# GpSimd's sums and differences of two SBUF operands moved to VectorE and ScalarE, three waits reordered

## The chip, the cores and the metric
The kernel runs on one core of a Trainium2 chip. The metric is the device time of one execution in microseconds; the time before is the median of three runs. PE (TensorE) multiplies matrices, VectorE (DVE in the rows) and GpSimd (POOL) and ScalarE (ACT) work element by element, and SyncE (SP) issues most transfers. PE's clock has two levels, 1.2 and 2.4 GHz; the profile gives the granted clock as a share of the higher one.

## The reference, cut to what matters
One inference step of a two-layer hybrid backbone for 640 tokens (512 latent ones and 128 of context) at width 1024, all in fp32:
```python
def modulate(x, g, shift, scale):
    return rmsnorm(x, g) * (1 + scale) + shift

def mixer_front(h, p):
    z = h @ p['w_in']
    a_b, a_c, a_x, sgu_uv, cq, ckv, k_pe, sq, sk, sv = split_in_proj(z)
    y_conv = a_b * dwconv_centred(a_c * a_x, p['conv_w'])
    y_sgu = chunk_sgu(sgu_uv, p['sgu_norm'], p['sgu_w'], p['sgu_b'])
    ...

def mix_latent(h, p, ckv_ctx, kpe_ctx, k_ctx, v_ctx):
    ...
    return jnp.concatenate([y_conv, y_sgu, y_mla, y_swa], axis=-1) @ p['w_out']

def squared_relu_mlp(h, w1, w2):
    return jnp.square(jax.nn.relu(h @ w1)) @ w2

def trunk_layer(x, mod, p, mix_fn):
    shift1, scale1, gate1, shift2, scale2, gate2 = jnp.split(mod, N_MOD, axis=-1)
    y, ctx_state = mix_fn(modulate(x, p['norm1'], shift1, scale1))
    x = x + gate1 * y
    x = x + gate2 * squared_relu_mlp(modulate(x, p['norm2'], shift2, scale2), p['w1'], p['w2'])
    return x, ctx_state
```
`mod` is silu(c) @ w_ada + b_ada, one vector of six parts for the latent tokens and one for the context. The MLP is 4096 wide. In sgu the second half of gelu(z) is normalised and mixed over chunks of 128 tokens by four matrices, and multiplies the first half. MLA and the windowed attention rotate parts of their queries and keys by position.

## The kernel before
**Precision.** Every fp32 operand of a product is kept as a high part, rounded to a shorter format, and a low part, the difference. `mm3` then makes three matrix products: high x high (L248), high x low (L249), low x high (L250). A weight unit is loaded by `load_unit`: a transfer into one of three raw buffers, the high part on ScalarE (L239), the low part (L240) on VectorE, or on GpSimd where `pool` is set, into one of four `hl` buffers. `split` (L253, L254) does the same for values made in the kernel.

**Layout.** Activations stand with features on the partitions, x as 128 x 8 x 640, and are worked through in two halves of 384 and 256 tokens. The result of a product stands in PSUM; banks come from three pools of two, `bank` takes the first two pools in turn and `bank2` the third.

**Order.** A scheduler puts each engine's instructions in one order when the program is built; an engine then works through its own list, and waits where an operand or a buffer isn't free yet. What stands ahead of an instruction on its engine is thus set beforehand.

**Start.** The sums of squares of x are made, then the normalised x (`xr`, L319, eight products of two SBUF operands on VectorE). The modulation vectors come from two sources: ada tiles, a 128x1024 weight block which two reductions on VectorE (L174) multiply with the two conditioning vectors and sum; and `AdaRows`, products on PE (`adar`, L198) of weights (`adan`, transfers L311 and L327) that are transposed back (`adat`, L210). Gains (L184), scaling on ScalarE and the low part of h (L337) follow. Then the first products of the input projection start.

**Attention half.** Three `tm_block` calls make token-major projections (`tm`), each with four weight units; in layer 0 their low parts are made on GpSimd. `tm_rstd` (L480, L482) makes the power -1/2 of the row norms on GpSimd. After that come sgu (four products, each evacuated by L582 on VectorE), the feature-major projection tiles (`fm`), rotation of queries and keys (L636 to L639), the windowed attention (the scaling by 1/sum is L731 on GpSimd), MLA (L942 subtractions, scaling L968), and the output projection `out`. Each of its tiles is added to x with a gate by `gate_add` (L428), which then adds the tile's squares to the norm's sum (L269 square on ScalarE, L270 sum).

**Second norm and MLP.** `Modulate.step` makes h per feature block and half: L358 scales x (VectorE), L365 makes the high part (ScalarE), L369 the low part (VectorE). The MLP begins with four W1 units loaded ahead (`head`, low parts on GpSimd) and two `Pair`s of hidden tiles: relu (L1140) and its square rounded (L1141) on ScalarE, the square in fp32 (L1145), and the low part (L1146). In layer 0 the remaining hidden tiles follow in `two_plain`, and the second product in `mlp2`; between them stand ada tiles for later use. Layer 1 makes part of its products by a block scheme with fewer products (`mod.sums` makes the sums of blocks that it needs).

## Time and profile before

| what | value |
|---|---|
| median of 3 runs | 1538.87 us (1536.42 to 1539.4) |
| the profiled execution, its own time | 1542.1 us |
| its span, first to last instruction | 1540.2 us |
| mean granted PE clock | 0.978 |

The rows further down come from the profiled execution, and its own time is what they add up to; it is 3.2 us above the median. In a row of grouped instructions the line is the kernel's line, "out<-in" names the tiles, x the number of instructions, and the first numbers after the bar are the busy time in us and the mean of one in ns. In a timeline the first column is the time since the start of the span and the second the duration; "[7.92 <-DMA ...]" is the idle time ahead of the instruction and what ended it.

### The profile page before, as it was taken

How to read it: one execution, taken by the hardware profiler on the slowest of the kernel's cores; microseconds unless marked ns; L12 is line 12 of the kernel's file. 1: busy time of each engine (PE TensorE's matmuls, PEld its weight loads, DVE VectorE, ACT ScalarE, POOL GpSimd, SP SyncE). 2: the span in 40 equal slices, each digit the busy share in tenths (PEclk: the TensorE clock that was granted, in tenths of full speed). 3: DMA queues.
4: the chain of work that ended last, by engine and by line, in shares of the span. 5: the costliest groups of instructions: out<-in, count | busy, mean ns of one | idle time of the engine just before them, and what ended most of it. 6: DMA issues, size and time to landing. Idle time of an engine off the chain costs nothing.

```text
span 1540.2 us, 25201 instructions
## 1 busy us (share of the span) xinstructions
PE 1477.7 (96%) x9716; PEld 1418.2 (92%) x9716; DVE 1129.9 (73%) x2210; ACT 668.4 (43%) x1400; POOL 242.9 (16%) x245
## 2 busy tenths in 40 slices
PE   6899999989999999999999999999999999999997
PEld 3798988889999999999999989898999999999996
DVE  5988877869978778776457666687886676566655
ACT  3544556744322322322236545675745244334422
POOL 2132103243210110110120120132300000000002
PEclk9899999999999999999999999999999999999999
DMA  8544321333654445444211411111223223222211
GB/s 312 202 134 139 99 67 35 102 101 100 204 161 155 151 139 163 151 150 138 80 49 57 128 43 35 36 49 45 83 69 96 69 83 96 62 76 96 84 55 69
DMA packets 50103, 160.22 MB, mean 104 GB/s; under 512 B 6208, under 2 KB 10304, under 8 KB 49984
## 3 DMA queue, kind: packets, MB, share of 16 engines
q1 hardware_dynamic: 48320, 154.68, 31.3%
q10 hardware_dynamic: 1664, 3.93, 0.7%
q8 instruction: 77, 1.26, 0.3%
q14 instruction: 42, 0.34, 0.1%
HBM read 155.55 MB, written 3.05 MB: 103 GB/s over the span
## 4 chain that ended last, share of the span: by engine, by line
PE 77%; DVE 10%; ACT 5%; issue 3%; POOL 1%; DMA 1%; POOLq 0%; DVEq 0%; ACTq 0%
PE w L250 13%; PE w L249 13%; PE w L248 13%; PE qcd L248 2%; PE fm L248 2%; PE qcd L250 2%; PE qcd L249 2%; PE fm L250 2%; PE fm L249 2%; PE out L248 2%; PE tm L249 2%; PE tm L248 2%; PE tm L250 2%; PE out L250 2%; PE out L249 2%
## 5 line engine op out<-in xcount | busy, mean ns | idle before, releaser
L248 PE MATMUL w<-u,hl 128*128 128x384 f32 (+1 forms) x1024 | 317.4, 310 | 5.7 <-DVE x L428 3.4
L249 PE MATMUL w<-u,hl 128*128 128x384 f32 (+1 forms) x1024 | 317.3, 310 | 0.7 <-DVE u L1198 0.7
L250 PE MATMUL w<-u,hl 128*128 128x384 f32 (+1 forms) x1024 | 317.1, 310 | 0.4 <-DVE hl L240 0.4
L239 ACT CAST hl<-raw 128x1024 fp32r<-128x1024 f32 (+3 forms) x176 | 170.6, 972 | 261.7 <-PE w L250 156.2
L240 DVE TENSOR_TENSOR hl<-raw,hl 128x1024 fp32r<-128x1024 f32 (+3 forms) x156 | 183.2, 1177 | 53.0 <-ACT hl L239 52.4
L428 DVE SCALAR_TENSOR_TENSOR x<-w,mod,x 128x128 f32<-128x128 f32 (+1 forms) x384 | 155.0, 434 | 73.1 <-PE w L250 71.8
L248 PEld LDWEIGHTS w<-u,hl 128*128 128x128 f32 x1024 | 194.6, 190 | 6.5 <-DVE x L428 3.6
L249 PEld LDWEIGHTS w<-u,hl 128*128 128x128 f32 x1024 | 194.8, 190 | 1.0 <-DVE u L1198 1.0
L250 PEld LDWEIGHTS w<-u,hl 128*128 128x128 f32 x1024 | 194.6, 190 | 0.6 <-DVE hl L240 0.6
L249 PE MATMUL w<-h,hl 128*128 128x384 f32 (+1 forms) x576 | 179.2, 313 | 3.6 <-DVE h L369 3.6
L250 PE MATMUL w<-h,hl 128*128 128x384 f32 (+1 forms) x576 | 179.4, 312 | 0.0
L248 PE MATMUL w<-h,hl 128*128 128x384 f32 (+1 forms) x576 | 179.0, 312 | 0.0
L174 DVE CUSTOM_DVE_ANT_0 junk<-adaw,cb,vec 128x1024 f32<-128x1024 f32 x84 | 110.5, 1317 | 28.2 <-DMA adaw<-in_wada 28.0
L270 POOL TENSOR_TENSOR ss<-ss,sq 128x384 f32<-128x384 f32 (+1 forms) x40 | 37.3, 932 | 504.7 <-ACT sq L269 503.9
L174 DVE CUSTOM_DVE_ANT_0 adaw<-adaw,cb,vec 128x1024 f32<-128x1024 f32 x84 | 114.2, 1359 | 1.1
L249 PEld LDWEIGHTS w<-h,hl 128*128 128x128 f32 x576 | 110.3, 192 | 4.8 <-DVE h L369 4.8
L1145 POOL TENSOR_TENSOR rq<-rr 128x384 f32<-128x384 f32 (+1 forms) x64 | 61.9, 969 | 334.2 <-ACT rr L1140 310.3
L248 PEld LDWEIGHTS w<-h,hl 128*128 128x128 f32 x576 | 110.5, 192 | 0.0
L250 PEld LDWEIGHTS w<-h,hl 128*128 128x128 f32 x576 | 110.3, 192 | 0.0
L248 PE MATMUL fm<-h,hl 128*128 128x256 f32 (+1 forms) x288 | 93.4, 324 | 2.1 <-DVE u L582 2.1
L249 PE MATMUL fm<-h,hl 128*128 128x256 f32 (+1 forms) x288 | 90.7, 315 | 0.0
L250 PE MATMUL fm<-h,hl 128*128 128x256 f32 (+1 forms) x288 | 90.6, 315 | 0.0
(329 smaller groups left out, 3404.6 us busy)
## 6 DMA issues: line engine op xcount, KB each, us to landing
raw<-in_wf SPq DMA_DIRECT2D x146, 512.0 KB, 3.5
adaw<-in_wada SPq DMA_DIRECT2D x84, 512.0 KB, 3.6
raw<-in_wo SPq DMA_DIRECT2D x24, 384.0 KB, 3.0
adan<-in_wnat SPq DMA_DIRECT2D x12, 512.0 KB, 8.3
raw<-in_wt SPq DMA_DIRECT2D x16, 384.0 KB, 3.3
x<-in_xT ACTq DMA_DIRECT2D x4, 640.0 KB, 7.2
raw<-in_wt SPq DMA_DIRECT2D x8, 288.0 KB, 3.0
raw<-in_wo SPq DMA_DIRECT2D x4, 512.0 KB, 3.6
```

The lines of the kernel that those rows point to most:

```text
L174: nc.vector.tensor_tensor_reduce(out=raw if g else junk, in0=raw, in1=cb[:, g, :], op0=ALU.mult, op1=ALU.add, scale=1.0, scalar=vecs[l][:, ...
L239: nc.scalar.copy(hl[:, 0, :n], raw[:, :n])
L240: (nc.gpsimd if pool else nc.vector).tensor_sub(hl[:, 1, :n], raw[:, :n], f(hl[:, 0, :n]))
L248: nc.tensor.matmul(out, lhsT=lhs[0], rhs=rhs[0], start=start, stop=False, skip_group_check=more)
L249: nc.tensor.matmul(out, lhsT=lhs[0], rhs=rhs[1], start=False, stop=False, skip_group_check=more)
L250: nc.tensor.matmul(out, lhsT=lhs[1], rhs=rhs[0], start=False, stop=stop, skip_group_check=more)
L270: (nc.gpsimd if pool else nc.vector).tensor_add(self.s[:, t0:t0 + n], self.s[:, t0:t0 + n], sq[:, :n])
L428: nc.vector.scalar_tensor_tensor(out=x[:, m, t0:t0 + n], in0=ps[:, t0 - b0:t0 - b0 + n], scalar=mods[l][g][:, gate + m:gate + m + 1], in1= ...
L1145: nc.gpsimd.tensor_mul(q, r, r)
```

## The change
All operations on GpSimd that take two SBUF tensors of some width are moved: the low parts of `load_unit` (20 on GpSimd before: eight of 768 columns and four of 576 in layer 0's `tm_block`, eight of 1024 in the `head` of both layers), the sums of the norm (20 of 384 columns and 20 of 256), the first product of the rotation (six), and the subtractions in MLA's queries (sixteen) go to VectorE. The 64 squares of layer 0's MLP go to ScalarE. The powers (L295, L482), four copies and the scalings by 1/sum (L731, L968) stay on GpSimd. Three orders change too: sgu puts two heads into one tile of the third PSUM pool; in `two_plain` of j = 1, seven ada tiles in place of eight are spread as (2, 2, 2, 1), and the last one comes later; in layer 1 the first W2 unit is loaded ahead of the block sums and handed to `mlp2`.

```diff
--- before.py
+++ after.py
@@ -232,12 +232,12 @@
                 ada_tile(*t, pool)
 
 
-    def load_unit(src, n=1024, pool=False):
+    def load_unit(src, n=1024):
         raw = rawp.tile([128, 1024], F32, tag="raw", name=nm("raw"))
         nc.sync.dma_start(out=raw[:, :n], in_=src)
         hl = hlp.tile([128, 2, 1024], F32R, tag="hl", name=nm("hl"))
         nc.scalar.copy(hl[:, 0, :n], raw[:, :n])
-        (nc.gpsimd if pool else nc.vector).tensor_sub(hl[:, 1, :n], raw[:, :n], f(hl[:, 0, :n]))
+        nc.vector.tensor_sub(hl[:, 1, :n], raw[:, :n], f(hl[:, 0, :n]))
         return hl
 
     def transpose(out, src):
@@ -261,13 +261,13 @@
             self.rb = None
             self.s = tp([128, TOK], "ss")
 
-        def add(self, k, t0, n, pool=False):
+        def add(self, k, t0, n):
             if k == 0:
                 nc.scalar.activation(self.s[:, t0:t0 + n], x[:, k, t0:t0 + n], AF.Square)
                 return
             sq = tmp2([128, 384], "sq")
             nc.scalar.activation(sq[:, :n], x[:, k, t0:t0 + n], AF.Square)
-            (nc.gpsimd if pool else nc.vector).tensor_add(self.s[:, t0:t0 + n], self.s[:, t0:t0 + n], sq[:, :n])
+            nc.vector.tensor_add(self.s[:, t0:t0 + n], self.s[:, t0:t0 + n], sq[:, :n])
 
         def start(self):
 
@@ -430,7 +430,7 @@
                 scalar=mods[l][g][:, gate + m:gate + m + 1], in1=x[:, m, t0:t0 + n],
                 op0=ALU.mult, op1=ALU.add)
         if norm is not None:
-            norm.add(m, *HALVES[half], m < 6)
+            norm.add(m, *HALVES[half])
 
 
     def layer(l, h, next_norm, nxt):
@@ -451,7 +451,7 @@
 
         def tm_block(srcs, kn, cols, evac):
             seq = (0, 1, 3, 2) if l == 0 else (0, 1, 2, 3)
-            us = {i: load_unit(srcs[i], kn * cols, l == 0) for i in seq}
+            us = {i: load_unit(srcs[i], kn * cols) for i in seq}
             ks = [i * kn + k for i in seq for k in range(kn)]
             if l == 0:
                 ada_steps(4, tt)
@@ -575,7 +575,9 @@
         ws = load_unit(wkvs[l, :, 512:1024], 512)
         wsH, wsL = (ws[:, s, 0:512].rearrange("p (h q) -> p h q", h=4) for s in range(2))
         for hd in range(4):
-            ps = bank("sgu")
+            if hd % 2 == 0:
+                two = bank2("sgu")
+            ps = two[:, hd % 2, :]
             d0 = 64 * hd
             mm3(ps[:, :320], (wsH[:, hd, :], wsL[:, hd, :]),
                 (vhl[0][:, :, d0:d0 + 64], vhl[1][:, :, d0:d0 + 64]), True, True)
@@ -634,7 +636,7 @@
             if i == 2:
                 nc.sync.dma_start(out=o_k[l], in_=xc[:, 2, :])
             nc.vector.stream_shuffle(out=tmp, in_=raw, mask=[z ^ 16 for z in range(32)])
-            nc.gpsimd.tensor_mul(raw, raw, rs[:, 0, :])
+            nc.vector.tensor_mul(raw, raw, rs[:, 0, :])
             nc.vector.tensor_mul(tmp, tmp, rs[:, 1, :])
             nc.vector.tensor_add(raw, raw, tmp)
             if i < 2:
@@ -939,7 +941,7 @@
                 for i in range(2):
                     r = ROPE[i]
                     nc.scalar.copy(qq[i][r, 0, t0:t0 + e], rot[r, :e])
-                    nc.gpsimd.tensor_sub(qq[i][r, 1, t0:t0 + e], rot[r, :e], f(qq[i][r, 0, t0:t0 + e]))
+                    nc.vector.tensor_sub(qq[i][r, 1, t0:t0 + e], rot[r, :e], f(qq[i][r, 0, t0:t0 + e]))
                     r = NOPE[i]
                     nc.scalar.activation(qq[i][r, 0, t0:t0 + e], pq[0][r, :e], AF.Copy, scale=MLA_SCALE)
                     nc.vector.scalar_tensor_tensor(
@@ -1139,10 +1141,7 @@
                 hh = ui[:, 0, t0:t0 + n]
                 nc.scalar.activation(r, ps[:, :n], AF.Relu)
                 nc.scalar.activation(hh, r, AF.Square)
-                if blocks:
-                    nc.scalar.activation(q, r, AF.Square)
-                else:
-                    nc.gpsimd.tensor_mul(q, r, r)
+                nc.scalar.activation(q, r, AF.Square)
                 nc.vector.tensor_sub(ui[:, 1, t0:t0 + n], q, f(hh))
 
             def load(self):
@@ -1237,7 +1236,7 @@
                 for half in range(2):
                     two[i // 2].plain([w, w], i % 2, half)
                 if l == 0:
-                    ada_steps((3, 3, 2, 0)[i] if j == 1 else 1)
+                    ada_steps((2, 2, 2, 1)[i] if j == 1 else 1)
             return two[0].u + two[1].u
 
         def mlp2_tile(ut, u, m, half, nrm):
@@ -1248,10 +1247,10 @@
                 mm3(ps[:, :n], (u[:, 0, c0:c0 + 128], u[:, 1, c0:c0 + 128]), act(ut, k, t0, n), k == 0, k == 3)
             gate_add(ps, m, half, l, 40, nrm)
 
-        def mlp2(j, ut):
+        def mlp2(j, ut, first=None):
             if j < 7:
                 for i in range(4):
-                    u = load_unit(wf[l, U_W2 + 4 * j + i])
+                    u = first if i == 0 and first else load_unit(wf[l, U_W2 + 4 * j + i])
                     for m in (2 * i, 2 * i + 1):
                         for half in range(2):
                             mlp2_tile(ut, u, m, half, None)
@@ -1269,7 +1268,7 @@
                     nxt.step(half, k)
 
         head = [Pair(p, None if blocks else [ta([128, 2, TOK], "u") for _ in range(2)]) for p in range(2)]
-        ws = [load_unit(wf[l, U_W1 + i], pool=True) for i in range(4)]
+        ws = [load_unit(wf[l, U_W1 + i]) for i in range(4)]
         for half in range(2):
             for i in range(4):
                 head[i // 2].plain(ws[2 * (i // 2):2 * (i // 2) + 2], i % 2, half)
@@ -1278,9 +1277,10 @@
                         mod.step(1, k)
         us = head[0].u + head[1].u
         if blocks:
+            first = load_unit(wf[l, U_W2])
             for s in range(4):
                 mod.sums(s)
-            mlp2(0, us)
+            mlp2(0, us, first)
             us = full(2) + full(3)
             for j in range(1, 8):
                 if j < 7:
```

The line numbers after the change are two higher from sgu on, and one lower than before behind the squares of the MLP.

The first place is VectorE's list at the start, right behind the eight L319; `adaw` and `junk` rows are the two reductions of an ada tile, `hl` the low parts of the first weight units. Before:
```order
L174 ISA adaw_289,mod_114<-adaw_289,cb,vec_92 128x1024
L174 ISA mod_114 128x1
L174 ISA junk_296,mod_114<-adaw_294,cb,vec_92 128x1024
L174 ISA mod_114 128x1
L174 ISA adaw_294,mod_114<-adaw_294,cb,vec_92 128x1024
L174 ISA mod_114 128x1
L184 SCALAR_TENSOR_TENSOR gain_116<-mod_114,vec_92 128x1
L174 ISA junk_303,mod_114<-adaw_301,cb,vec_92 128x1024
```
And after:
```order
L174 ISA adaw_289,mod_114<-adaw_289,cb,vec_92 128x1024
L174 ISA mod_114 128x1
L174 ISA junk_296,mod_114<-adaw_294,cb,vec_92 128x1024
L174 ISA mod_114 128x1
L240 TENSOR_TENSOR hl_407<-raw_405,hl_407 128x768
L174 ISA adaw_294,mod_114<-adaw_294,cb,vec_92 128x1024
L174 ISA mod_114 128x1
L184 SCALAR_TENSOR_TENSOR gain_116<-mod_114,vec_92 128x1
L174 ISA junk_303,mod_114<-adaw_301,cb,vec_92 128x1024
```
The first low part stands two reductions' rows behind `adaw_289`, which was and is followed by the same reduction. The three others stand further down, all ahead of the first L337, and one reduction (`adaw_430`) moves behind six of the L337.

The second place is VectorE's list in layer 0's second norm, at the end of half 0: `mt`, `h` are the blocks of the norm, `ss` and `sq` its sum, `out` the output projection. Before:
```order
L358 SCALAR_TENSOR_TENSOR mt_3611<-x,gain_117,rb_3506 128x384
L369 SCALAR_TENSOR_TENSOR h_3605<-mt_3606,mod_114,h_3605 128x384
L358 SCALAR_TENSOR_TENSOR mt_3616<-x,gain_117,rb_3506 128x384
L369 SCALAR_TENSOR_TENSOR h_3610<-mt_3611,mod_114,h_3610 128x384
L358 SCALAR_TENSOR_TENSOR mt_3621<-x,gain_117,rb_3506 128x384
L369 SCALAR_TENSOR_TENSOR h_3615<-mt_3616,mod_114,h_3615 128x384
L293 TENSOR_SCALAR nst_3685<-rb_3682 128x2
L174 ISA junk_4036,mod_114<-adaw_4034,cb,vec_92 128x1024
L174 ISA mod_114 128x1
L369 SCALAR_TENSOR_TENSOR h_3620<-mt_3621,mod_114,h_3620 128x384
```
And after:
```order
L240 TENSOR_TENSOR hl_3636<-raw_3634,hl_3636 128x1024
L369 SCALAR_TENSOR_TENSOR h_3558<-mt_3559,mod_114,h_3558 128x384
L369 SCALAR_TENSOR_TENSOR h_3563<-mt_3564,mod_114,h_3563 128x384
L270 TENSOR_TENSOR ss_3290<-ss_3290,sq_3600 128x256
L358 SCALAR_TENSOR_TENSOR mt_3604<-x,gain_117,rb_3504 128x384
L358 SCALAR_TENSOR_TENSOR mt_3609<-x,gain_117,rb_3504 128x384
L358 SCALAR_TENSOR_TENSOR mt_3614<-x,gain_117,rb_3504 128x384
L369 SCALAR_TENSOR_TENSOR h_3603<-mt_3604,mod_114,h_3603 128x384
L369 SCALAR_TENSOR_TENSOR h_3608<-mt_3609,mod_114,h_3608 128x384
L369 SCALAR_TENSOR_TENSOR h_3613<-mt_3614,mod_114,h_3613 128x384
L358 SCALAR_TENSOR_TENSOR mt_3619<-x,gain_117,rb_3504 128x384
L240 TENSOR_TENSOR hl_3641<-raw_3639,hl_3641 128x1024
```
Behind these rows follow the last `h_3618` and the fourth low part. Three of the four low parts of the head stand ahead of the last block of half 0 and no ada reduction does; the ten sums stand ahead of it too, the five wide ones further up, before the half's L293.

The third place is PE's list behind the third tm block, where `sgu` and `fm` are as above, three rows for each `mm3`. Before, the fourth sgu product and the first of fm:
```order
L248 MATMUL sgu_1073<-vhl_400,hl_1055 128x320
L249 MATMUL sgu_1073<-vhl_401,hl_1055 128x320
L250 MATMUL sgu_1073<-vhl_400,hl_1055 128x320
L248 MATMUL fm_1116<-h_130,hl_1108 128x384
L249 MATMUL fm_1116<-h_130,hl_1108 128x384
L250 MATMUL fm_1116<-h_130,hl_1108 128x384
```
And after, from the first sgu product:
```order
L248 MATMUL sgu_1058<-vhl_400,hl_1055 128x320
L249 MATMUL sgu_1058<-vhl_401,hl_1055 128x320
L250 MATMUL sgu_1058<-vhl_400,hl_1055 128x320
L248 MATMUL fm_1114<-h_130,hl_1106 128x384
L249 MATMUL fm_1114<-h_130,hl_1106 128x384
L250 MATMUL fm_1114<-h_130,hl_1106 128x384
```
Before, the four sgu products stood together and fm behind them; now fm's products begin behind the first, and the other three stand among them.

## Rows read from the trace of the kernel before
**Rows 1.** The page's first part: busy us of each engine, share, instructions.
```profile
PE 1477.7 (96%) x9716; PEld 1418.2 (92%) x9716; DVE 1129.9 (73%) x2210; ACT 668.4 (43%) x1400; POOL 242.9 (16%) x245
```
**Rows 2.** Busy us (instructions) of PE, weight loads, DVE, ACT, POOL; clock; DMA, by stretch.
```profile
25.00:425.00 400.00, 369.70 (x2315) 337.48 (x2314) 344.94 (x690) 203.69 (x488) 112.23 (x96) 0.95 0.38 122
425.00:800.00 375.00, 375.00 (x2553) 375.00 (x2552) 264.99 (x480) 98.13 (x159) 49.37 (x54) 1.00 0.43 135
```
**Rows 3.** PE's waits: instruction, what ended them, total us, times, longest.
```profile
PE adar L198 <- DMA adan<-in_wnat: 7.9, 1, 7.9
...
PE w L249 <- DVE h L369: 3.6, 3, 2.4
PE w L248 <- DVE x L428: 3.4, 1, 3.4
...
PE tm L249 <- POOL hl L240: 2.3, 1, 2.3
...
PE fm L248 <- DVE u L582: 2.1, 1, 2.1
...
PE w L248 <- ACT hl L239: 1.6, 1, 1.6
```
**Rows 4.** Span and mean granted clock of the core.
```profile
core 0: 1540.2 us, clock 0.978
```
**Rows 5.** The same view: four stretches at the half clock.
```profile
99.20:102.60 3.40, 3.40 (x15) 3.40 (x16) 3.40 (x4) 0.58 (x1) 2.71 (x2) 0.50 0.72 236
348.40:355.20 6.80, 6.38 (x22) 6.29 (x22) 6.71 (x10) 3.20 (x5) 3.19 (x2) 0.50 0.41 145
416.70:423.50 6.80, 5.86 (x21) 5.86 (x22) 6.80 (x15) 1.04 (x1) 0.00 (x0) 0.50 0.63 227
...
1095.90:1099.30 3.40, 3.40 (x13) 3.40 (x12) 3.08 (x5) 2.49 (x5) 1.62 (x2) 0.50 0.68 243
```
**Rows 6.** Instructions by line and shape, whole run, VectorE and ScalarE.
```profile
L254 DVE TENSOR_TENSOR hl<-s,hl 128x1024 fp32r<-128x1024 f32 x28 | 34.3, 1226 | 16.0 <-ACT hl L253 15.9
L240 DVE TENSOR_TENSOR hl<-raw,hl 128x768 fp32r<-128x768 f32 x32 | 30.8, 964 | 3.8 <-ACT hl L239 3.6
L369 DVE SCALAR_TENSOR_TENSOR h<-mt,mod,h 128x384 fp32r<-128x384 f32 x24 | 22.1, 936 | 0.7 <-ACT h L365 0.6
L358 DVE SCALAR_TENSOR_TENSOR mt<-x,gain,rb 128x384 f32<-128x384 f32 x24 | 14.0, 602 | 2.0 <-PE rb L297 2.0
L319 DVE TENSOR_TENSOR xr<-x,rbs 128x640 f32<-128x640 f32 x8 | 12.4, 1622 | 0.0
L270 DVE TENSOR_TENSOR ss<-ss,sq 128x384 f32<-128x384 f32 x15 | 8.3, 556 | 5.8 <-ACT sq L269 5.8
L337 DVE TENSOR_TENSOR h<-xr,h 128x640 fp32r<-128x640 f32 x8 | 6.2, 819 | 0.0
...
L1141 ACT ACTIVATE u<-rr 128x384 fp32r<-128x384 f32 x36 | 18.9, 525 | 0.9
```
**Rows 7.** The same for VectorE from 25 to 425 us alone.
```profile
L174 DVE CUSTOM_DVE_ANT_0 adaw<-adaw,cb,vec 128x1024 f32<-128x1024 f32 x41 | 56.9, 1387 | 0.6
...
L240 DVE TENSOR_TENSOR hl<-raw,hl 128x1024 fp32r<-128x1024 f32 x21 | 28.4, 1356 | 3.6 <-ACT hl L239 3.5
...
L369 DVE SCALAR_TENSOR_TENSOR h<-mt,mod,h 128x384 fp32r<-128x384 f32 x8 | 9.6, 1214 | 0.2 <-ACT h L365 0.2
```
**Rows 8.** Timelines of the start: SP's queue, VectorE, PE.
```profile
38.56 3.96 SPq L327 DMA_DIRECT2D adan<-in_wnat  x4
37.26 1.27 DVE L174 CUSTOM_DVE_ANT_0 adaw<-adaw,cb,vec 128x1024 f32<-128x1024 f32 x1
42.10 1.87 PE L198 MATMUL adar<-adan,cs 128*2 128x256 f32 x4 [7.92 <-DMA adan<-in_wnat]
```
**Rows 9.** Timelines around 930 us: GpSimd's scaling and a low part on VectorE.
```profile
930.47 0.70 POOL L731 TENSOR_SCALAR P<-P,as 128x512 f32<-128x512 f32 x1 [0.78 <-DVE as L730]
930.62 1.35 DVE L240 TENSOR_TENSOR hl<-raw,hl 128x768 fp32r<-128x768 f32 x1 [0.34 <-ACT hl L239]
```

## The prediction

> **What bounds the kernel now.** I read the page's busy times first, then busy time by stretch, then the waits of PE, then the clock. PE is busy 1477.7 us, VectorE 1129.9, GpSimd 242.9 [rows 1]. GpSimd is far from a bound, so work taken off it gives nothing by itself; it can only give what it makes others wait for. In the MLP of layer 0 (425 to 800 us) PE is busy in all 375 us, and VectorE has 110 us to spare; from 25 to 425 us PE is busy 369.7 of 400 and VectorE 344.9 [rows 2]. So the time lies in two kinds of place. One is PE's waits [rows 3]: none is longer than 7.9 us, and they stand at the start, in the attention half of a layer, and at the second norm and the start of an MLP. The other is the clock: its mean is 0.978 [rows 4], and [rows 5] shows four stretches at the half clock (granted 0.50, the 1.2 GHz level). Three begin within 2 us of one of those waits; in the fourth, at 1095.9, PE had waited in the second norm of layer 1. A stretch of 6.8 us at 0.50 does the work of 3.4, so it costs 3.4 more; the ones of 3.4 us cost 1.7.
>
> What GpSimd does to VectorE is seen in pairs of rows of equal size [rows 6]. L319 multiplies two SBUF operands of 128x640 in 1622 ns, and L337, which subtracts two of the same size, takes 819; L319 runs while GpSimd makes four low parts. L369 (two SBUF operands) takes 936 ns in the mean, against 602 for L358 of the same width, one of whose operands stands in PSUM. In 25 to 425 us L369 takes 1214, and the 1024-wide low part (L240) 1356 [rows 7], against 1226 for its undisturbed twin L254 [rows 6]. Those VectorE operations are long where GpSimd runs one with two operands.
>
> **The change part by part.** *Work added to VectorE.* Priced at the undisturbed rows of [rows 6]: 8 low parts of 1024 at 1.23 (9.8 us), 8 of 768 at 0.96 (7.7), 4 of 576 at three quarters of that (2.9), 20 sums of 384 at 0.56 (11.1), 20 of 256 at two thirds of it (7.4), 6 rotations of 512 at four fifths of L337's 0.82 (4.0), 8 subtractions of 384 columns at 0.56 (4.4) and 8 of 128 at a third (1.5): 49 us. From 25 to 425 us it is 4 of the 1024-wide, all of the 768 and 576, 10 sums, half of the rotations and of the subtractions: 25 us. One ada tile fewer stands there, two reductions of 1.39 [rows 7], 2.8 us. So +22 on an engine with 55 to spare.
>
> *What comes back to VectorE there.* L319 8 x (1.62 - 0.82) = 6.4 us [rows 6]; L369 8 x (1.21 - 0.60) = 4.9; the 1024-wide low parts 21 x (1.356 - 1.226) = 2.7 [rows 6, 7]. That is 14 from rows with a clean twin; smaller groups add to it. VectorE ends some us busier than before there, but its work stands earlier.
>
> *Squares to ScalarE.* 64 operations in layer 0's MLP at 0.525 us for the wide ones (L1141) [rows 6] and two thirds for the narrow: 28 us onto an engine busy 98 of 375 [rows 2]. Without that cover the price would be 28; with PE at 375 of 375 I take nothing, within a lower end of nothing too.
>
> Now by place, with a value, and both ends.
>
> A. *Start.* The four adan transfers reuse buffers that the ada reductions free; the last of these runs 37.26 to 38.53, the transfers start at 38.56, and adar on PE follows at 42.10 [rows 8] after 7.9 us of waiting [rows 3]. Behind L319's 6.4 us the reductions move up by that much; the new L240 stand behind the one that frees the buffers, as the order rows show, so they don't delay it, but all four (3.9 us) stand ahead of the first h, with one ada reduction (1.3) moved away. Ends: 6.4, and 6.4 less the 3.9 plus nearly nothing, 3. I take **5**: the chain there runs through the transfers and PE, not through VectorE's total.
>
> B. *Third tm block.* PE waits 2.3 us for a low part on GpSimd [rows 3], which stands behind two powers (L482); then come 3.4 us of half clock [rows 5], 1.7. Now VectorE makes it right behind L480. From 0 (VectorE comes no earlier) to 4; I take **3**.
>
> C. *sgu.* With two heads in a bank of another pool, fm's first tile no longer waits for the last sgu tile's evacuation, 2.1 us [rows 3]. From 0 to 4 (with a half-clock stretch of 1.7 behind it); **2**.
>
> G. *Second norms.* PE waits 3.6 us for h of L369, in both layers together [rows 3]; half clock at 348.4 and 1095.9 costs 3.4 + 1.7 [rows 5]. Upper end 8.7. Against it stand, ahead of the last h of half 0, three new low parts (3.7) and ten sums (4.6), 8.3 us a layer, in layer 0 less the 1.3 of the ada reduction: 15.3 in all. L369 gives back 4.9 in layer 0, and at least half of the other 8.0 - 4.9 in layer 1, 6.4 in all; the five wide sums of each layer (5.6) stand ahead of L293, where VectorE still waits for the output projection's products. 15.3 - 6.4 - 5.6 leaves 3.3 later as the lower end. I take **4.5**: about half of each wait and of each half-clock stretch.
>
> H. *Start of layer 0's MLP.* PE waits 3.4 for L428 [rows 3], whose results free PE's banks, and the half clock at 416.7 costs 3.4 [rows 5]. VectorE is then busy all of 6.80 us [rows 5], with ada reductions ahead. One tile fewer there is 2.8, and held-up low parts come back. Lower end 2.8, upper 6.8; **6**.
>
> M. *Layer 1.* PE's one wait of 1.6 for a high part (L239) [rows 3]: the unit is now loaded ahead of the block sums. 0 to 1.6; **1.6**.
>
> J. *The rest:* rotation, subtractions in MLA, half clock elsewhere: 1540.2 x 0.022 = 33.9 us are lost to the clock in all [rows 4], 10.2 of them in the four stretches. From 0 to 6 (a quarter of the other 24); **1.5**, because the moved operations there go onto VectorE's list, too.
>
> Sum: 5 + 3 + 2 + 4.5 + 6 + 1.6 + 1.5 = 23.6. The profiled execution took 1542.1 us, 3.2 above the median of 1538.87. 1542.1 - 23.6 = 1518.5, less 3.2: **1515**. The lower ends sum to 3 + 2.8 - 3.3 = 2.5, 1536.4; the upper ones to 37.5, 1501.4.
>
> **The rivals.**
> *VectorE becomes the bound of the first 420 us.* The +22 eats what comes back; only A and H give, 5 + 6: 1542.1 - 11 - 3.2 = **1528**. For it: VectorE is at 86% there [rows 2], and full at 348 and 416 [rows 5]. Against it: the sum counts the added work only where it stands ahead of a wait.
>
> *The scalings left on GpSimd (L731, L968) hold VectorE.* GpSimd's started at 930.47 and ran 0.70; a VectorE low part that began at 930.62 took 1.35 [rows 9], against 0.96 [rows 6]. If each of the 22 rotations and subtractions now on VectorE meets one so, that is 8.6, half of it on the path: **1520**. The Trainium skill, "SBUF — State Buffer", Who interferes with whom, has it that of a VectorE operation with two SBUF inputs and a GpSimd one that reads SBUF, whichever started second is blocked until the first ends. By that rule it would be 0.55 here (930.62 to 931.17), 12 for all 22, and 1521; the trace agrees that it was held, by 0.39. It also speaks against hoping that all of VectorE's excess goes.
>
> *All waits go, and more clock with them:* every upper end, **1501** or less. For it: [rows 5] all stand beside waits that the change touches. Against: VectorE's extra work.
>
> *Nothing measurable:* the lower ends, **1536**, within 0.2% (3.1 us, about what a measurement here can tell). It needs A and H alone, with the second norms late.
>
> *Slower.* One mechanism: the second norms. If nothing comes back there, h is late by the whole 15.3 us, with A and H at their lower ends, 5.8, giving 1542.1 + 15.3 - 5.8 - 3.2 = **1548**. It decides from where less than 5.8 of the 15.3 is left uncovered. L369's 6.4 us to return [rows 6, 7] and the wide sums' place speak against it.
>
> **How the numbers follow.** Forecast (1505 to 1525) 0.58; scalings 0.06; VectorE as bound 0.18 (1524 to 1535); all waits 0.10; nothing 0.04; slower 0.04. The first four are faster by over 0.2%: 0.92. The likeliest gives 1515; from 1500 to 1530 lie the forecast, the scalings, two thirds of the VectorE case and half of the last fast case: 0.58 + 0.06 + 0.12 + 0.05 = 0.81.
>
> **What would show it.** A: L319 at about 0.82, adan transfers some 6 us earlier, the first tm product near 49. B, C: PE's waits for hl and u gone, 0.95 in the clock from 25 to 425 up. G: L369 at 0.60, PE's wait for it under 2 us and no 6.8 us at 0.50 at about 325 to 335. H: no wait for L428 at the MLP's start. GpSimd at some 70 to 110 us. The MLP of layer 0 stays full, with ScalarE 28 us busier. Wrong if the second norm shows PE waiting longer for h, or if half-clock stretches appear at new places.

## The result and the profile after

The changed kernel takes 1516.7 us (median of four runs, 1516.33 to 1517.54), against 1539.13 for the kernel before in the same comparison: a ratio of 0.9847, with a 95% interval of 0.9827 to 0.9867 (estimated from the runs of both; the quotient of the two medians is 0.9854). The forecast was 1515, between 1500 and 1530. The profiled execution took 1516.33 us, 25.8 less than the profiled one of before (1542.1), against a forecast sum of 23.6.

The page's busy times after, which answer to [rows 1]:
```profile
PE 1463.1 (97%) x9716; PEld 1403.2 (93%) x9716; DVE 1130.4 (75%) x2292; ACT 692.0 (46%) x1464; POOL 75.7 (5%) x99
```
VectorE has 82 more instructions and 0.5 us more to do. At the clean rows of the changed kernel the moved operations cost it 50.9 us, so 50.4 us have come back: that long it had been held up. PE does the same 9716 products in 14.6 us less, and is idle for 1514.3 - 1463.1 = 51.2 us, against 62.5 before: 11.3 less. So more than half of the 25.9 us that the span lost is products that ran faster: by the trace's clock PE was busy for 54.2 us at the half clock before, and for 19.1 after. The core's span and mean clock, as [rows 4]:
```profile
core 0: 1514.3 us, clock 0.990
```
1514.3 x 0.010 = 15.1 us are lost to the clock, over idle and busy time, against 33.9 before. Busy time by stretch, the two of [rows 2], then places of [rows 5], then two where the half clock is still granted:
```profile
25.00:425.00 400.00, 382.94 (x2479) 351.85 (x2478) 352.49 (x756) 215.23 (x512) 38.53 (x43) 0.98 0.41 130
425.00:800.00 375.00, 373.20 (x2536) 372.34 (x2536) 269.15 (x515) 123.52 (x228) 2.19 (x2) 1.00 0.40 129
...
98.60:102.00 3.40, 3.40 (x28) 3.40 (x27) 3.40 (x6) 2.48 (x13) 0.00 (x0) 1.00 0.27 100
347.00:354.00 7.00, 7.00 (x53) 6.93 (x52) 6.81 (x24) 5.43 (x17) 0.00 (x0) 1.00 0.00 0
415.00:422.00 7.00, 7.00 (x47) 7.00 (x46) 6.17 (x14) 1.41 (x2) 0.00 (x0) 1.00 0.50 152
...
204.40:211.20 6.80, 5.31 (x25) 4.53 (x25) 4.70 (x15) 4.44 (x14) 1.42 (x2) 0.52 0.05 13
941.80:945.20 3.40, 3.40 (x18) 2.78 (x19) 1.83 (x6) 2.02 (x6) 0.98 (x2) 0.52 0.07 19
```
PE now does more in the first 400 us, and the three places that had 0.50 are at 1.00. The last two rows, still at the half clock, stand in the attention of the two layers. PE's waits, as [rows 3]:
```profile
PE rb L290 <- DVE ss L270: 5.9, 4, 3.4
PE rb L297 <- POOL nst L295: 3.5, 4, 1.3
PE out L248 <- ACT ymla L253: 2.7, 2, 1.3
PE adar L198 <- DMA adan<-in_wnat: 2.6, 2, 2.3
PE pt L244 <- POOL P L733: 2.2, 4, 1.1
...
PE w L248 <- DVE x L428: 1.2, 1, 1.2
...
PE sgu L248 <- DVE u L584: 1.0, 2, 0.5
...
PE tm L249 <- DVE hl L240: 0.7, 1, 0.7
...
PE w L249 <- DVE h L369: 0.6, 3, 0.2
```
The wait of 7.9 us for adan is 2.6; the 3.6 for h are 0.6; those for a low part on GpSimd, for ScalarE's high part and that of fm for u are gone, though sgu now waits 1.0 for its own u. Two others in the attention grew: for `ymla` (1.3 before) and for P, scaled on GpSimd (0.2 before). The 3.4 us for L428 are gone from layer 0 (the 1.2 that stand here are in layer 1). The VectorE groups of [rows 6]:
```profile
L240 DVE TENSOR_TENSOR hl<-raw,hl 128x1024 fp32r<-128x1024 f32 x124 | 151.9, 1226 | 55.7 <-ACT hl L239 55.3
L369 DVE SCALAR_TENSOR_TENSOR h<-mt,mod,h 128x384 fp32r<-128x384 f32 x24 | 14.1, 614 | 0.9 <-ACT h L365 0.6
L319 DVE TENSOR_TENSOR xr<-x,rbs 128x640 f32<-128x640 f32 x8 | 6.0, 819 | 0.0
```
L319 takes exactly its twin's 819 ns, L369 614 instead of 936. At the start, timelines of SP's queue and of PE, as [rows 8]:
```profile
32.42 0.33 SPq L327 DMA_DIRECT2D adan<-in_wnat  x1
34.49 0.33 SPq L237 DMA_DIRECT2D raw<-in_wt  x1
34.92 1.59 SPq L327 DMA_DIRECT2D adan<-in_wnat  x3
36.27 1.65 PE L198 MATMUL adar<-adan,cs 128*2 128x256 f32 x6 [2.30 <-DMA adan<-in_wnat]
49.09 0.45 PE L248 MATMUL tm<-hl,h 128*128 128x384 f32 x1 [0.22 <-ACT h L336]
```
The transfers start 6.1 us earlier (32.42 for 38.56), adar 5.8, the first tm product 4.9 (49.09 for 53.97). The last three adan transfers now have a weight transfer in front of them.

The same work cut into segments on PE shows where the time went. Each segment ends where the trace shows the start of a product: the first tm, the last tm of the layer, the last out, the first tm of layer 1 (for layer 1: the last w), and the last product of all. In us:

| segment | before | after | e1 | e2 | e3 | e9 | e10 | e4 | e5 |
|---|---|---|---|---|---|---|---|---|---|
| start | 53.97 | 49.09 | 47.79 | 54.86 | 55.79 | 55.60 | 48.85 | 48.14 | 47.83 |
| tm blocks, layer 0 | 62.51 | 57.57 | 57.58 | 62.52 | 62.50 | 62.50 | 57.56 | 57.57 | 57.61 |
| attention, layer 0 | 226.96 | 224.12 | 225.55 | 225.05 | 223.33 | 226.33 | 225.91 | 222.85 | 222.11 |
| second norm and MLP, layer 0 | 465.23 | 453.67 | 453.66 | 462.55 | 461.43 | 454.29 | 462.61 | 453.60 | 459.11 |
| tm blocks, layer 1 | 59.35 | 60.91 | 60.90 | 59.35 | 60.91 | 60.91 | 60.88 | 59.36 | 60.93 |
| attention, layer 1 | 220.08 | 217.97 | 217.09 | 218.50 | 216.93 | 219.21 | 218.11 | 216.37 | 217.03 |
| second norm and MLP, layer 1 | 440.60 | 439.01 | 443.33 | 439.09 | 441.02 | 440.51 | 441.20 | 437.37 | 438.99 |
| end | 4.17 | 4.98 | 4.61 | 4.15 | 4.98 | 4.98 | 4.98 | 4.16 | 5.01 |

Between kernels that are equal there the attention of layer 0 moves by up to 4 us, the start, the attention of layer 1 and its MLP by 1 to 3, the MLP of layer 0 by 0.7, and the tm blocks and the end by 0.4 at most. In layer 1 the movement goes with the half clock: its MLP takes 439.0 without a stretch of it (the changed kernel, e5) and 440.5 with one of 3.4 us (e9). After against before: -4.9, -4.9, -2.8, -11.6, +1.6, -2.1, -1.6, +0.8. Two segments became longer.

The two attention segments as windows, before and then after:
```profile
116.48:343.44 226.96, 214.69 (x1421) 198.01 (x1420) 185.32 (x416) 127.25 (x315) 57.33 (x60) 0.97 0.29 90
868.02:1088.10 220.08, 214.18 (x1421) 198.26 (x1420) 156.77 (x348) 128.60 (x316) 51.45 (x60) 0.97 0.18 56
...
106.66:330.78 224.12, 211.34 (x1421) 195.52 (x1419) 189.39 (x436) 127.33 (x313) 32.53 (x37) 0.98 0.29 91
846.36:1064.33 217.97, 210.31 (x1420) 194.17 (x1418) 162.22 (x371) 127.79 (x314) 26.03 (x37) 0.99 0.18 56
```
PE is idle there for 12.3 and 5.9 us before, and for 12.8 and 7.7 after. What these two segments gained is clock, not waiting.

### The profile page after: what moved, and what is told of

Its sections match the earlier page's. It is cut to its first block, busy times and chain, and to the rows that moved or that the text cites. A ratio compares the mean times of both kernels' runs of the same rounds, so it can differ in the third digit from the quotient of the medians.

```text
span 1514.3 us, 24982 instructions
## 1 busy us (share of the span) xinstructions
PE 1463.1 (97%) x9716; PEld 1403.2 (93%) x9716; DVE 1130.4 (75%) x2292; ACT 692.0 (46%) x1464; POOL 75.7 (5%) x99
## 4 chain that ended last, share of the span: by engine, by line
PE 82%; DVE 8%; ACT 5%; DMA 2%; issue 2%; POOL 1%; POOLq 0%; SPq 0%; DVEq 0%; ACTq 0%
PE w L250 15%; PE w L249 15%; PE w L248 14%; PE tm L248 2%; PE tm L249 2%; PE tm L250 2%; PE qcd L248 2%; PE qcd L250 2%; PE qcd L249 2%; PE fm L248 2%; PE out L248 2%; PE fm L250 2%; PE fm L249 2%; PE out L249 2%; PE out L250 2%
## 5 line engine op out<-in xcount | busy, mean ns | idle before, releaser
L249 PE MATMUL w<-u,hl 128*128 128x384 f32 (+1 forms) x1024 | 315.8, 308 | 0.7 <-DVE u L1197 0.7
L240 DVE TENSOR_TENSOR hl<-raw,hl 128x1024 fp32r<-128x1024 f32 (+3 forms) x176 | 199.4, 1136 | 61.6 <-ACT hl L239 60.6
L428 DVE SCALAR_TENSOR_TENSOR x<-w,mod,x 128x128 f32<-128x128 f32 (+1 forms) x384 | 155.3, 434 | 59.9 <-PE w L250 58.6
L249 PEld LDWEIGHTS w<-u,hl 128*128 128x128 f32 x1024 | 193.6, 189 | 1.0 <-DVE u L1197 1.0
L249 PE MATMUL w<-h,hl 128*128 128x384 f32 (+1 forms) x576 | 178.1, 310 | 0.7 <-DVE h L369 0.6
L249 PEld LDWEIGHTS w<-h,hl 128*128 128x128 f32 x576 | 109.0, 189 | 1.7 <-DVE h L369 1.5
L248 PEld LDWEIGHTS w<-h,hl 128*128 128x128 f32 x576 | 108.8, 189 | 1.4 <-ACT h L365 1.3
L250 PEld LDWEIGHTS w<-h,hl 128*128 128x128 f32 x576 | 109.0, 189 | 0.2
L174 DVE CUSTOM_DVE_ANT_0 adaw<-adaw,cb,vec 128x1024 f32<-128x1024 f32 x84 | 107.9, 1285 | 0.7
L248 PE MATMUL fm<-h,hl 128*128 128x256 f32 (+1 forms) x288 | 91.3, 317 | 0.0
L249 PE MATMUL fm<-h,hl 128*128 128x256 f32 (+1 forms) x288 | 89.1, 309 | 0.0
L250 PE MATMUL fm<-h,hl 128*128 128x256 f32 (+1 forms) x288 | 89.1, 309 | 0.0
L249 PE MATMUL tm<-hl,h 128*128 128x384 f32 (+1 forms) x240 | 77.3, 322 | 0.7 <-DVE hl L240 0.7
L1142 ACT ACTIVATE rr<-w 128x384 f32<-128x384 f32 (+1 forms) x72 | 31.3, 435 | 101.3 <-PE w L250 101.3
```

What stands on the lines that cost most here:

```text
L174: nc.vector.tensor_tensor_reduce(out=raw if g else junk, in0=raw, in1=cb[:, g, :], op0=ALU.mult, op1=ALU.add, scale=1.0, scalar=vecs[l][:, ...
L240: nc.vector.tensor_sub(hl[:, 1, :n], raw[:, :n], f(hl[:, 0, :n]))
L248: nc.tensor.matmul(out, lhsT=lhs[0], rhs=rhs[0], start=start, stop=False, skip_group_check=more)
L249: nc.tensor.matmul(out, lhsT=lhs[0], rhs=rhs[1], start=False, stop=False, skip_group_check=more)
L250: nc.tensor.matmul(out, lhsT=lhs[1], rhs=rhs[0], start=False, stop=stop, skip_group_check=more)
L428: nc.vector.scalar_tensor_tensor(out=x[:, m, t0:t0 + n], in0=ps[:, t0 - b0:t0 - b0 + n], scalar=mods[l][g][:, gate + m:gate + m + 1], in1= ...
```

## The experiments

The theory was that GpSimd's operations with two SBUF operands held up VectorE's, so that taking them off it is most of the gain. One rival was that the three new orders carry it; another that GpSimd was only slow itself, and what waited was what needed its results.

**e1: the moves without the new orders.**
```diff
-            if hd % 2 == 0:
-                two = bank2("sgu")
-            ps = two[:, hd % 2, :]
+            ps = bank("sgu")
...
-                    ada_steps((2, 2, 2, 1)[i] if j == 1 else 1)
+                    ada_steps((3, 3, 2, 0)[i] if j == 1 else 1)
...
-            mlp2(0, us, first)
+            mlp2(0, us)
```


> The changed kernel with its three reorders undone: sgu takes banks in turn again, the ada tiles stand (3, 3, 2, 0) again, layer 1's first W2 unit is loaded behind the block sums again; all operations stay off GpSimd. Theory (GpSimd's two-operand operations held VectorE up, and freeing it is most of the gain): about 1523 us (1519 to 1527), the 2 us of sgu, some 3 of the ada tile and 1.6 of the W2 unit lost, the start and the third tm block unchanged. Rival (the reorders carry the gain): 1533 or more.

1521.25 us (ratio to before 0.9879, 0.9854 to 0.9905). The moves carry 18.5 us (1539.71 for the kernel before in that comparison) of the 22.4; the interval overlaps that of the changed kernel, so the rest isn't clear of the noise in this run. Of the orders only one shows by itself: layer 1's MLP is 4.3 us longer (443.33 for 439.01; kernels with the new order have up to 441.2), at PE's wait for the first W2 unit:
```profile
PE w L248 <- ACT hl L239: 3.8, 1, 3.8
```
It was 1.6 before [rows 3]; a half clock of 6.8 us stands behind it. The ada order makes no difference once the moves are made (453.66).

**e2: the new orders alone** (those three edits on the kernel before).

> The kernel before with the three reorders alone; GpSimd keeps all its operations. Theory (holding): about 1533 us (1530 to 1537), first tm product still near 54 us, the 6.8 us of half clock in the second norm still there. Rival (the reorders carry the gain): 1523 or less.

1535.92 us (0.9974, 0.996 to 0.9989): 3.8 us less than before. The start, the tm blocks and VectorE's rows from 23 to 425 us are those of before:
```profile
L319 DVE TENSOR_TENSOR xr<-x,rbs 128x640 f32<-128x640 f32 x8 | 12.4, 1623 | 0.0
L369 DVE SCALAR_TENSOR_TENSOR h<-mt,mod,h 128x384 fp32r<-128x384 f32 x8 | 9.6, 1214 | 0.2 <-ACT h L365 0.2
```
So the first rival falls. Without the moves the ada order is worth 2.7 us (462.55 for 465.23).

**e3: the 20 low parts back on GpSimd.**
```diff
-        nc.vector.tensor_sub(hl[:, 1, :n], raw[:, :n], f(hl[:, 0, :n]))
+        (nc.gpsimd if pool else nc.vector).tensor_sub(hl[:, 1, :n], raw[:, :n], f(hl[:, 0, :n]))
...
-            us = {i: load_unit(srcs[i], kn * cols) for i in seq}
+            us = {i: load_unit(srcs[i], kn * cols, l == 0) for i in seq}
...
-        ws = [load_unit(wf[l, U_W1 + i]) for i in range(4)]
+        ws = [load_unit(wf[l, U_W1 + i], pool=True) for i in range(4)]
```


> The changed kernel with the 20 low parts of weights on GpSimd again (tm blocks of layer 0, heads of both MLPs). Theory (holding): the eight L319 take 1.6 us each again, the first tm product is back near 54 (from 49.1), the third tm block waits again, the second norms' L369 are long again: about 1531 us (1526 to 1536). Rival (GpSimd was only slow itself, 2.4 us for a unit against 1.0, and what waits is what needs its results): the start stays at 49, since it waited for transfers; only the third tm block loses its 5: 1521 to 1523.

1537.32 us (0.9986, 0.9972 to 0.9999): nearly all of the gain is gone, 6 us more than expected and beyond the range that I gave. 20 of the 82 operations that moved to VectorE decide it.

**e9 and e10: the same by halves,** first the twelve of the tm blocks, then the eight of the heads.

> The changed kernel with only the twelve low parts of layer 0's tm blocks on GpSimd again. By the segments of the runs so far (start, tm blocks, the rest), holding is local: start 5 us longer, tm blocks of layer 0 62.5 in place of 57.6, and the second norm with the MLP of layer 0 unchanged at 453.7: about 1526 us (1523 to 1530). Rival (the losses of the version with all 20 back came through VectorE's whole list, not locally): the MLP of layer 0 gets longer too, by over 2 us.

> The changed kernel with only the eight 1024-wide low parts of the two MLP heads on GpSimd again. Local holding: start 48 to 49 and tm blocks 57.6 unchanged, the second norm with the MLP of layer 0 about 461 in place of 453.7, with layer 1's 2 us longer: 1526 us (1522 to 1529). Rival as before: start or tm blocks change by over 2 us.

e9: 1532.14 us (0.9933, 0.9913 to 0.9954), 6 more than expected and outside the range given. Start +6.5, tm blocks +4.9, MLP of layer 0 +0.6, as the theory has it; the other 5 us lie in both attentions and layer 1's MLP, which the edit doesn't touch. Each of the three has 3.4 us more of half clock than in the changed kernel, worth 1.7 us each: the first and the last of these rows are new, and the middle one stands for the 3.4 us at 941.8 there.
```profile
150.00:153.40 3.40, 3.40 (x13) 3.40 (x14) 2.61 (x7) 1.37 (x3) 1.15 (x2) 0.50 0.48 154
...
955.50:962.30 6.80, 6.28 (x28) 5.54 (x28) 3.18 (x9) 2.61 (x9) 1.28 (x2) 0.50 0.03 10
1102.30:1105.70 3.40, 3.40 (x16) 3.40 (x17) 3.37 (x8) 3.40 (x8) 0.00 (x0) 0.50 0.00 0
```
Why they came stays open; in layer 1's MLP e6, whose code there is the changed kernel's, has one too (at 1085.1). VectorE at the start and PE's wait in the third block:
```profile
L319 DVE TENSOR_TENSOR xr<-x,rbs 128x640 f32<-128x640 f32 x8 | 12.4, 1623 | 0.0
...
PE tm L249 <- POOL hl L240: 2.3, 1, 2.3
```
e10: 1526.92 us (0.9901, 0.9879 to 0.9923). Start and tm blocks as after; second norm and MLP +8.9 in layer 0, +2.2 in layer 1. From 325 to 360 us L369 is long again, and from 325 on PE waits:
```profile
L369 DVE SCALAR_TENSOR_TENSOR h<-mt,mod,h 128x384 fp32r<-128x384 f32 x8 | 7.4, 948 | 0.1
...
PE w L248 <- DVE x L428: 2.4, 2, 1.6
```
The loss stays where the GpSimd operations stand.

**e4: the 40 sums back on GpSimd.**
```diff
-            nc.vector.tensor_add(self.s[:, t0:t0 + n], self.s[:, t0:t0 + n], sq[:, :n])
+            (nc.gpsimd if pool else nc.vector).tensor_add(self.s[:, t0:t0 + n], self.s[:, t0:t0 + n], sq[:, :n])
...
-            norm.add(m, *HALVES[half])
+            norm.add(m, *HALVES[half], m < 6)
```


> The changed kernel with the 40 sums of the norms on GpSimd again. Theory (holding): each sum of 1.0 or 0.85 us on GpSimd holds VectorE's two-operand operations in the second norms and at the layers' ends, the price of which is about what VectorE saves by not making them (18 us in all): 1518 us (1515 to 1521). Rival (GpSimd is only slow itself): nobody waits for these sums, and VectorE is relieved: 1511 to 1514.

1510.79 us (0.9809, 0.9794 to 0.9823): faster than the changed kernel, against my theory and for its rival. The sums' 19.5 us leave VectorE, and its busy time falls by 18.3, so GpSimd's sums hold VectorE up next to nothing:
```profile
PE 1459.8 (97%) x9716; PEld 1403.0 (93%) x9716; DVE 1112.1 (74%) x2252; ACT 690.9 (46%) x1464; POOL 112.5 (7%) x139
```
The reason stands in the rows of their neighbour, the gated sum L428, which reads a product from PSUM: 613 ns in the kernel with GpSimd's sums (first row, e4) and 613 in the one without (second, the changed kernel).
```profile
L428 DVE SCALAR_TENSOR_TENSOR x<-w,mod,x 128x384 f32<-128x384 f32 x128 | 78.4, 613 | 37.6 <-PE w L250 37.4
```
```profile
L428 DVE SCALAR_TENSOR_TENSOR x<-w,mod,x 128x384 f32<-128x384 f32 x128 | 78.5, 613 | 28.1 <-PE w L250 27.9
```
Only a few of these 128 run beside a sum, so single ones say more. In e4's trace, an L428 wholly beside a sum, then an L369, which has two SBUF operands, beside another:
```profile
306.83 1.02 POOL L270 TENSOR_TENSOR ss<-ss,sq 128x384 f32<-128x384 f32 x1 [10.19 <-ACT sq L269]
307.07 0.62 DVE L428 SCALAR_TENSOR_TENSOR x<-out,mod,x 128x384 f32<-128x384 f32 x1 [0.41 <-PE out L250]
...
778.41 0.74 POOL L270 TENSOR_TENSOR ss<-ss,sq 128x256 f32<-128x256 f32 x1 [2.25 <-ACT sq L269]
778.40 1.16 DVE L369 SCALAR_TENSOR_TENSOR h<-mt,mod,h 128x384 fp32r<-128x384 f32 x1
```
L428 takes its 0.62, L369 1.16 in place of 0.61. Of the 37.3 us of GpSimd's sums in e4, 14.0 run beside L428, 17.1 while VectorE does nothing, 4.6 beside L240 and L369, and most of the rest beside L358, which reads PSUM too.

Both segments that had become longer are back at before's values: tm blocks of layer 1 59.36, the end 4.16. PE's wait for the norm at layer 1's start, in the changed kernel and in e4:
```profile
PE rb L297 <- POOL nst L295: 1.1, 1, 1.1
...
PE rb L297 <- POOL nst L295: 0.3, 1, 0.3
```
The 0.7 for a low part (tm L249, in the waits of the changed kernel) stands there too, and is gone in e4. Moving the sums was a loss.

**e5: the 64 squares back on GpSimd.**
```diff
-                nc.scalar.activation(q, r, AF.Square)
+                if blocks:
+                    nc.scalar.activation(q, r, AF.Square)
+                else:
+                    nc.gpsimd.tensor_mul(q, r, r)
```


> The changed kernel with the 64 squares of layer 0's MLP on GpSimd again. PE is full in that MLP, so a difference can only come at its start. First theory (GpSimd's two-operand work beside VectorE's ada reductions and low parts delays the gated sums at the MLP's start, and with them PE's banks): the wait for L428 is back with a stretch of half clock: 1519 us (1517 to 1523). Rival (ScalarE's 28 us were the dearer place, or neither matters): 1515 to 1517.

1518.25 us (0.9855, 0.9826 to 0.9884): by the times not to be told from the changed kernel. The segment tells more: the MLP of layer 0 is 5.4 us longer, and PE's wait at its start is back, while start and attention came out 3.3 us shorter, which this edit doesn't touch.
```profile
PE w L248 <- DVE x L428: 2.2, 1, 2.2
```

**e6: rotation and MLA's subtractions back on GpSimd** (`nc.gpsimd` again in those two lines).

> The changed kernel with the rotation's first product and the sixteen subtractions of MLA on GpSimd again. What the sums showed (a GpSimd operation costs nothing where VectorE's neighbours have an operand in PSUM): the subtractions stand beside L945, which reads PSUM, so they are free on GpSimd, and the rotations stand beside L638 and low parts, which they hold up by about 1.5 + 3.3 us in the trace of before; VectorE saves 10 us. In sum 1514 to 1518, most likely 1516. Rival (any two-operand work on GpSimd costs): 1519 or more.

1519.77 us (0.9855, 0.9829 to 0.9882): outside the range that I gave, at the rival's. But the ratio is that of the changed kernel within its interval, and the profiled execution, the fastest of the four, has the changed kernel's span (1514.2). So no effect is clear of the noise, and the run doesn't decide between the two.

**e7: eight products of two SBUF operands on GpSimd beside L319,** and **e8: twelve scalings with one.** Both outputs go to a spare buffer.
```diff
+        spare = tmp2([128, 384], "spare")
+        for k in range(KT):
+            nc.gpsimd.tensor_mul(spare, x[:, k, :384], norm.rb[:, :384])
         for k in range(KT):
             nc.vector.tensor_mul(ts[k], x[:, k, :], norm.rb)
```
In e8 the loop is `for k in range(12)` with `nc.gpsimd.tensor_scalar(out=spare, in0=norm.rb[:, :384], ...)`.

> The changed kernel with eight products of two SBUF operands (384 columns) put on GpSimd while VectorE makes the eight L319; the products go to a spare buffer and nobody reads them. Holding by pairs of two-operand work: L319 is long again (1.3 to 1.7 us each in place of 0.82) and the first tm product is 3 to 5 us later, near 53. Rival (the low parts' own lateness set the start): L319 stays at 0.82, first tm product near 49.

> The changed kernel with twelve scalings of one SBUF operand (384 columns) on GpSimd at the same place; nobody reads them. Holding by the rule that any GpSimd operation that reads SBUF blocks VectorE's two-operand ones: L319 at 1.2 to 1.7 us, first tm product at 52 to 54. Rival (only two-operand operations on GpSimd hold much): L319 under 1.0, first tm product within 1 us of 49.

Single times: 1523.72 and 1520.47. In e7, by timelines, one of the held VectorE operations, the first GpSimd one, with nothing of L319 beside it, and the one before the held:
```profile
24.58 1.62 DVE L322 TENSOR_TENSOR xr<-x,rbs 128x640 f32<-128x640 f32 x1
19.70 0.99 POOL L320 TENSOR_TENSOR spare<-x,rbs 128x384 f32<-128x384 f32 x1 [1.62 <-ACT rbs L281]
...
23.98 1.54 POOL L320 TENSOR_TENSOR spare<-x,rbs 128x384 f32<-128x384 f32 x1
```
And in e8:
```profile
24.52 1.12 DVE L323 TENSOR_TENSOR xr<-x,rbs 128x640 f32<-128x640 f32 x1
19.78 0.51 POOL L320 TENSOR_SCALAR spare<-rbs 128x384 f32<-128x384 f32 x1 [1.64 <-ACT rbs L281]
...
23.94 1.03 POOL L320 TENSOR_SCALAR spare<-rbs 128x384 f32<-128x384 f32 x1
```
Alone L319 takes 0.82. Beside a two-operand product it takes 1.62, and the product 1.54 in place of 0.99; beside a scaling 1.12, and the scaling 1.03 in place of 0.51. The two engines take turns, so each pays for the other's operation. Counted from the first of them, VectorE's eight operations end 3.2 and 1.5 us later. The first tm product stands at 52.32 (+3.2) and 49.27 (+0.2, less than the start moves by itself). In e7 nobody needed GpSimd's results, so the second rival falls for the start. e8 bears out neither of its two expectations in full: the first tm product is where the rival had it, but L319 is held, by less than its theory had. "SBUF — State Buffer", Who interferes with whom, in the Trainium skill describes this as a pair of ports which one of the two engines has until its operation ends. The turns of e7 agree with it, though VectorE is held there for 0.80 us by an operation of 0.99.

**e11: sums and MLA's subtractions on GpSimd, all else as changed.**

> The changed kernel with the sums of the norms and MLA's sixteen subtractions on GpSimd again: the operations whose VectorE neighbours (L428, L945) mostly have an operand in PSUM. If the neighbour decides, both are free on GpSimd: 1509 to 1512 us, first tm block of layer 1 at 59.4 (60.9 in the changed kernel), the end after the last MLP product 4.2 (5.0). Rival (any two-operand work on GpSimd costs, and the version with the sums back was fast for another reason): over 1514.

1511.12 us (0.9794, 0.9773 to 0.9815); tm blocks of layer 1 59.37, the end 4.52. As fast as e4; both beat both kernels, and their intervals lie below the changed kernel's.

What each group had cost VectorE can be estimated from the busy times of the versions that put it back: the change in busy time, plus the group's own work that left. Low parts 1140.8 - 1130.4 + 20.6 = 31.0 us; squares 1139.3 - 1130.4 = 8.9; rotation and subtractions 1126.1 - 1130.4 + 10.8 = 6.5; sums 1112.1 - 1130.4 + 19.5 = 1.2. Together 47.6 of the 50.4.

## Why the prediction was right

- **Direction and size.** 25.8 us against 23.6, by the mechanism that was named. The prediction let VectorE end busier by 8 us from 25 to 425 (+22 for the new work, -14 for what comes back); it was 7.6 (352.49 for 344.94). That the sum came so near is in part luck: B was sized too low and two losses (1.6 and 0.8) were not forecast; and 3.4 of the 25.8 is only that the profiled execution of before was a long one, as the medians differ by 22.4.
- **A, the start:** 5 forecast, 4.9 measured, along the chain that was named; e7 takes 3.2 of them back by work that nobody needs.
- **B, the third tm block:** mis-sized. 3 forecast with an upper end of 4; 4.9 measured: 62.5 in every kernel with these low parts on GpSimd, 57.6 to 57.9 in the others. The wait for GpSimd's low part and the half clock behind it (2.3 + 1.7) were all of my upper end; a shorter wait ahead of them, for ScalarE, and the rest of the gaps went too.
- **C and J, attention:** 3.5 forecast, 2.8 + 2.1 measured, but not by the waits that were named. fm's wait of 2.1 is gone, yet PE's idle time in the two segments is 0.5 and 1.8 longer, since sgu's, `ymla`'s and P's waits came in its place. The gain is half clock: 13.7 us of it before in each attention, 6.8 and 3.4 after. How much of that the change made is not shown, as these segments move by as much by themselves. By e6 the rotation and the subtractions are worth nothing that shows; by e2 the segments are shorter by 1.9 and 1.6 with the orders alone, which is no more than they move.
- **G and H, second norms and MLP:** 10.5 forecast, with M 12.1; 11.6 + 1.6 = 13.2 measured. The reason was right in kind (L369 at 614, no half clock at 347 and 415), but the parts are not a sum: undoing the heads' low parts alone costs 8.9 in layer 0, the squares alone 5.4, together more than the 11.6, since either brings a wait and a stretch of half clock back. I had given H to the ada tile and the low parts; e1 shows that the ada order gives nothing once the rest is done, and e5 that the squares, to which I had given no gain, count in this MLP.
- **M:** 1.6 forecast for a wait of 1.6. On the kernel before the order is worth that (e2: 439.09 for 440.60). With the moves made and without it the wait is 3.8 and the segment 2 to 4 us longer; why the wait grew was not tried. But little of the 1.6 is left of it against the kernel before: among the first W2 products the changed kernel waits 1.2 for L428 and 0.6 for a low part, where the kernel before waited 1.6 and 0.4. The segment's own -1.6 has the stretch of half clock at 1095.9 in it, which is gone and was worth 1.7.
- **The step that failed most** is the price of the sums. The prediction saw them ahead of the last h of the second norm and nowhere else, and took them for part of what holds VectorE. They hold up next to nothing, as most of them run beside L428, which reads PSUM, or while VectorE is idle; and at each layer's end, where no stall comes back, they delay the next norm: +1.6 and +0.8, both gone in e4 and nearly so in e11; the second norm and MLP of layer 1 is 1.6 shorter there, too. Together that is 4.0 us of the 5.9 by which e4's median is lower; the rest lies in the segments that move by themselves.
- **The rivals.** VectorE did not become the bound, although it is busy 352 of 400 us. The scalings do hold VectorE, by 0.30 us each beside L319 in e8, but what that costs did not show in the first tm product there.
- **Two slips in the working** moved no forecast. A's lower end is 2.5 by its own figures (6.4 less 3.9), or 3.8 with the reduction moved away, and not 3. The slower rival needs more than 5.8 of the 15.3 uncovered, not less.

## What to carry to other kernels

Before moving an operation off GpSimd, look at what VectorE does beside it: with two SBUF operands on both engines, the two take turns, and the move can cost VectorE less than the hold did (the low parts: 20.6 us of work against 31.0). Beside a VectorE operation that reads PSUM, or where VectorE was idle, GpSimd's work was free and the move costs its full price. Price a short wait on PE by the granted clock behind it as well: here 14.6 of 25.9 us came from products that ran faster. Undo a change group by group: 20 of the moved operations carried it, and 40 of them were a loss.

## What the runs showed of the hardware

A scaling of one operand holds VectorE as well, only for less: 0.30 us for one of 0.51 us, against 0.80 for a two-operand product of 0.99 us. GpSimd pays in turn beside an L319: 0.52 us on the scaling, 0.55 on the product. An operation on VectorE that reads one operand from PSUM was not held: L428 took 0.62 us wholly beside a GpSimd sum.
